# Token phase of a streaming encoder step: the queues of its stores, the unit in which its keys are transposed, and the tiles of the rotation's scratch

## The chip, the core and the metric

The kernel runs on one core of a Trainium2 chip. The metric is the device time of one execution in microseconds (us), as a median of several runs. Work is spread over TensorE (PE; PEld is its weight load), VectorE (DVE), ScalarE (ACT), GpSimd (POOL) and SyncE (SP). Each engine takes its instructions in a fixed order, and a transfer is started by an instruction in the queue of SP, ACT or POOL.

## The reference, cut to what matters

One layer over 4096 prompt frames and 32 sample frames, all in float32:

```python
h = rmsnorm(x, norm_g)
proj = jnp.einsum('bsd,de->bse', h, w_in)
q, k, v, ga, u, gp = jnp.split(proj, [...], axis=-1)
q = rope(q.reshape(B, S, N_HEADS, 2, HEAD_DIM), pos)      # 4 heads, two 64-wide halves each
k = rope(k.reshape(B, S, N_HEADS, 2, HEAD_DIM), pos)      # k and v are outputs too
o = diff_attention(q, k_all, v_all, pos, kpos_all, lam)   # block-causal
o = rmsnorm(o, subln_g, SUBLN_EPS) * (1.0 - lam_init)
a_out = o.reshape(B, S, ATTN_WIDTH) * jax.nn.silu(ga)
p_out = pool_mix(u, pool_hist, pos, w_pool, pool_scale) * jax.nn.silu(gp)
y = x + jnp.einsum('bse,ed->bsd', jnp.concatenate([a_out, p_out], axis=-1), w_out)
y = rmsnorm(y, final_g)
```

Outputs are y, the rotated keys, the values and the last pooling rows, for the prompt and for the sample.

## The kernel before, in words

Four phases follow each other: the token phase (`token_phase`: queries, keys and values of all tokens), the channel phase (gates and pooling), attention, and the output projection. Only the token phase is touched by the change; in the profile it lies between 0 and about 560 us. What it makes goes to scratch in DRAM, from where attention loads it.

A float32 product is made of three matmuls over a high and a low part of each operand (`mm3`, L112 to L114), so a projection over the 1024 inputs is 8 steps of three matmuls. Tokens come in nine spans (`SPANS`, mostly 512 tokens, four blocks of 128). For each span there are units of 24 matmuls: four q units, then a k unit for each block, then a v unit for each block. A unit writes a PSUM tile of the pool `two`, which has three buffers (`bank`), so the PSUM tile of a unit must have been read before the third unit after it can start.

The steps that the prediction speaks of:

- `norm_in`, `norm`: a block of rows is loaded (xn, L247), ACT squares and sums it (L252), DVE makes the reciprocal of the mean (L253, L254), and ACT its root (rx, L255). `scales_out` (L259) writes the 128 values of a block, one from each partition, to `rx_scr`; `scales` (L221) reads them back spread over all partitions (bc).
- `x_parts` loads two 128-row pieces of the transposed input (x, L205), and ACT and DVE split them (L108, L109). `ahead` places these loads and splits of the next span among the units of the current one.
- `q_out`: DVE scales the sums (z, L275), rotates the first tile with the help of two ACT copies (L278, L279), ACT and DVE split it into hi and lo, and both are stored (L288).
- `keys_out`: ACT scales the sums into kt (L299), POOL rotates 16 of each 64 columns in place (L304 to L307, with the scratch rot), and kt is stored (L308). `keys_across`: PE transposes kt in four pieces into the one PSUM tile `tp` (L314), ACT and DVE split it (L108, L109), and hi and lo are stored (L319).
- `values_out`: ACT scales the sums into v (L325), which is stored twice (L326, L327).
- `load_piece` (L237 to L239): a piece of weights is loaded, and ACT and DVE split it.

A k unit or a v unit begins with six of its eight steps, then calls `across` (which transposes all keys held so far) and ends with the two last steps. So the keys of a unit are transposed within the unit that follows it.

All stores and loads of this phase are started from SP. The tiles kt, rot, hi, lo, z, zs, v and bc share the eight buffers of one tag of the pool `sm`; the row and input tiles (xn, x before its split, tab) share four buffers of the pool `st`. The framework orders each engine's instructions when the program is built. The transfers of SP (and of ACT, where it starts any) share eight completion semaphores, and a transfer that is given one waits at its queue's head until the previous transfer on it has landed; POOL's transfers have others.

Of the kernel before, what the change touches and what calls it, by code (L numbers as in the profile page):

```python
# [11 lines left out]
F32 = mybir.dt.float32  # L12
# [8 lines left out]
P = 128  # L21
# [6 lines left out]
NB = SEQ // P  # L28
NH = 4
# [38 lines left out]
def encoder(tc, a, o):  # L68
    nc = tc.nc
    V, S, G, T = nc.vector, nc.scalar, nc.gpsimd, nc.tensor  # L70
    dma = nc.sync.dma_start
    rdma = nc.gpsimd.dma_start
    with ExitStack() as es:
        def pool(name, bufs, **kw):
            return es.enter_context(tc.tile_pool(name=name, bufs=bufs, reuse_waits="tile", **kw))
# [9 lines left out]
        q_scr = dram.tile([NH * 2, 2, 64, TOK], F32R, name="q_scr")  # L85
        rx_scr = dram.tile([1, TOK], F32, name="rx_scr")
        k_scr = dram.tile([NH, 2, 2, 64, TOK], F32R, name="k_scr")
        v_scr = dram.tile([NH, P, NB + 1, P], F32, name="v_scr")
# [12 lines left out]
        def s_tile(shape, dt=F32, name="s"):  # L101
            return sm.tile(shape, dt, tag="s", name=name)
# [4 lines left out]
        def split(hi, lo, src):  # L107
            S.copy(hi, src)  # L108
            V.tensor_sub(lo, src, hi)  # L109
# [9 lines left out]
        def p2_tile(name):  # L119
            return two.tile([P, 1024], F32, tag="two", name=name)  # L120

        def p1_tile(tag, name):
            return one.tile([P, 512], F32, tag=tag, name=name)
# [36 lines left out]
        etiny = early.enter_context(tc.tile_pool(name="etiny", bufs=2, reuse_waits="tile"))  # L160
        cs = econst.tile([P, NB + 1, 2, 8], F32, name="cs")
        rx = const.tile([P, NB + 1], F32, name="rx")
# [62 lines left out]
        def token_phase():  # L225
# [15 lines left out]
            def blocks(sp):  # L241
                t0, n = sp[:2]
                return [(t, min(P, t0 + n - t)) for t in range(t0, t0 + n, P)]
# [12 lines left out]

            def scales_out(t0, n):
                for t, m in blocks((t0, n)):
                    dma(rx_scr[0:1, t:t + m].rearrange("o t -> t o"), rx[:m, t // P:t // P + 1])  # L259

            def table(t0, n):
                tab = st.tile([P, 2, 512], F32, tag="st", name="tab")
# [8 lines left out]
            def q_out(ps, sp, i, bc, tab):  # L271

                t0, n = sp[:2]
                z = s_tile([P, 512], name="z")
                V.scalar_tensor_tensor(z[:, :n], ps[:, :n], 0.125, bc[:, :n], op0=ALU.mult, op1=ALU.mult)  # L275
                if i == 0:
                    zs = s_tile([P, 512], name="zs")
                    S.copy(zs[0:64, :n], z[64:128, :n])  # L278
                    S.copy(zs[64:128, :n], z[0:64, :n])  # L279
                    V.tensor_mul(z[:, :n], z[:, :n], tab[:, 0, :n])  # L280
                    V.tensor_mul(zs[:, :n], zs[:, :n], tab[:, 1, :n])
                    V.tensor_add(z[:, :n], z[:, :n], zs[:, :n])
                hi = s_tile([P, 512], F32R, name="hi")
                lo = s_tile([P, 512], F32R, name="lo")
                split(hi[:, :n], lo[:, :n], z[:, :n])
                for l, t in ((0, hi), (1, lo)):
                    for p0, p1, d in ((0, 64, 0), (64, 128, 8)) if i == 0 else ((0, P, i * 16),):
                        dma(q_scr[:, l, d:d + (p1 - p0) // 8, t0:t0 + n].rearrange("g d t -> g d t").bitcast(F32),  # L288
                            t[p0:p1, :n].bitcast(F32))

            def project(ps, sp, t0, m, kind, k):
                c = slice(t0 - sp[0], t0 - sp[0] + m)
                xh, xl = sp[2:4]
                mm3(ps[:m], xh[k][:, c], xl[k][:, c], w[kind][k][0], w[kind][k][1], k == 0, k == NK - 1)

            def keys_out(ps, t0, m):
                b = t0 // P
                kt = s_tile([P, 512], name="kt")
                S.activation(kt[:m], ps[:m], AF.Copy, scale=rx[:m, b:b + 1])  # L299
                ab = kt[:m].rearrange("t (g d) -> t g d", d=64)[:, :, 0:16].rearrange("t g (z f) -> t g z f", z=2)  # L300
                rot = s_tile([P, 2, 8, 2, 8], name="rot")
                rc, rs = rot[:m, 0], rot[:m, 1]
                bc = lambda i: cs[:m, b, i].unsqueeze(1).unsqueeze(1).to_broadcast([m, 8, 2, 8])
                G.tensor_mul(rc, ab, bc(0))  # L304
                G.tensor_mul(rs, ab, bc(1))
                G.tensor_sub(ab[:, :, 0], rc[:, :, 0], rs[:, :, 1])
                G.tensor_add(ab[:, :, 1], rc[:, :, 1], rs[:, :, 0])  # L307
                dma(o["k_prompt"][t0:t0 + m, :] if b < NB else o["k_sample"], kt[:m])  # L308
                return t0, m, kt

            def keys_across(t0, m, kt):
                tp = p1_tile("tp", "tp").rearrange("p (h t) -> p h t", h=NH)
                for h in range(NH):
                    T.transpose(tp[:, h, :m], kt[:m, h * P:(h + 1) * P], ident[:m, :m])  # L314
                hi = s_tile([P, NH, P], F32R, name="hi")
                lo = s_tile([P, NH, P], F32R, name="lo")
                split(hi[:, :, :m], lo[:, :, :m], tp[:, :, :m])
                for l, t in ((0, hi), (1, lo)):
                    dma(k_scr[:, l, :, :, t0:t0 + m].rearrange("h j d t -> (j d) h t").bitcast(F32),  # L319
                        t[:, :, :m].bitcast(F32))  # L320

            def values_out(ps, t0, m):
                b = t0 // P
                v = s_tile([P, 512], name="v")
                S.activation(v[:m], ps[:m], AF.Copy, scale=rx[:m, b:b + 1])  # L325
                dma(o["v_prompt"][t0:t0 + m, :] if b < NB else o["v_sample"], v[:m])  # L326
                dma(v_scr[:, :m, b].rearrange("h t e -> t h e"), v[:m].rearrange("t (h e) -> t h e", h=NH))  # L327

            def bank():
                return p2_tile("ps")[:, 0:512]  # L330

            held = []

            def across():
                while held:
                    keys_across(*held.pop(0))

            def q_unit(sp, i):
                ps = bank()
                for k in range(NK):  # L340
                    q_sum(ps, sp, i, k)
                q_out(ps, sp, i, *sp[4])

            def k_unit(sp, t):
                ps = bank()
                for k in range(NK):
                    if k == 6:
                        across()
                    project(ps, sp, *t, 1, k)
                held.append(keys_out(ps, *t))  # L350

            def v_unit(sp, t):
                ps = bank()
# [25 lines left out]
            def run(units, *jobs):  # L379
                for u, unit in enumerate(units):  # L380
                    for j in jobs:
                        for f in j.pop(u, []):
                            f()
                    unit()
                for j in jobs:
                    for u in sorted(j):
                        for f in j[u]:
                            f()


            t0, n = SPANS[0]
# [18 lines left out]
            bl = blocks(sp)  # L410
# [9 lines left out]
            both = p2_tile("ps")  # L420
# [3 lines left out]
            for t, xn in zip(bl, xns):  # L424
                norm(*t, xn)
            scales_out(t0, n)
            for k in range(NK):
                load_piece(2, k)
            for i in range(2):
                held.append(keys_out(both[:, i * 512:i * 512 + 512], *bl[i]))  # L430

            def rest():
                extra.extend([scales(t0, n), table(t0, n)])
# [6 lines left out]
            for s in range(1, len(SPANS) - 2):  # L440
# [7 lines left out]
                bl = blocks(sp)  # L448
# [174 lines left out]

        channel = channel_phase()
        last_channels = channel.send(token_phase())


# [358 lines left out]
        def out_half(yp, w, hl, m, n, k):  # L986
            r = slice(n * 512, (n + 1) * 512)
            mm3(yp[:m, :512], hl[:, 0, k, :m], hl[:, 1, k, :m], w[k][0][:, r], w[k][1][:, r], k == 0, k == 3)

        class PoolPart:  # L990
# [26 lines left out]
            def unit(self):  # L1017

                t0, m, hl, xn = self.blocks[0]
                if self.x == 0:  # L1020
                    self.yp = p2_tile("yp")
                for x in range(self.x, self.x + UNIT):
                    out_half(self.yp[:, x // 4 * 512:], self.w, hl, m, x // 4, x % 4)
                    if x == 7:
                        V.tensor_add(xn[:m], self.yp[:m], xn[:m])  # L1025
                self.x = (self.x + UNIT) % 8
                self.left -= 1
                if self.x == 0:
                    dma(x_scr[t0:t0 + m, :], xn[:m])
                    self.blocks.pop(0)  # L1030
                    if self.seq:
                        self.blocks.append(self.load())
                return UNIT * 0.64
# [185 lines left out]
```

## Time and profile before

| what | us |
|---|---|
| median of 3 runs (2866.47 to 2874.34) | 2867.46 |
| the profiled execution | 2871.01 |
| its span | 2869.2 |
| PE busy in the span (97%) | 2769.3 |
| PE waiting between 40 and 500 us, all of it for a key's tile or its bank | 48.2 |

The page's first part has PE busy in 97% of the span, and its second part shows the slices in which it was not. The share is a mean over four phases, so the stretch of the token phase is to be read by itself. A time in the rows is counted from the span's start.

### The profile page before, as it was taken

How to read it: one execution, taken by the hardware profiler on the slowest of the kernel's cores; microseconds unless marked ns; L12 is line 12 of the kernel's file. 1: busy time of each engine (PE TensorE's matmuls, PEld its weight loads, DVE VectorE, ACT ScalarE, POOL GpSimd, SP SyncE). 2: the span in 40 equal slices, each digit the busy share in tenths (PEclk: the TensorE clock that was granted, in tenths of full speed). 3: DMA queues.
4: the chain of work that ended last, by engine and by line, in shares of the span. 5: the costliest groups of instructions: out<-in, count | busy, mean ns of one | idle time of the engine just before them, and what ended most of it. 6: DMA issues, size and time to landing. Idle time of an engine off the chain costs nothing. (4 is left out here: it accounts for less than half of the span.)

```text
span 2869.2 us, 42987 instructions
## 1 busy us (share of the span) xinstructions
PE 2769.3 (97%) x15719; PEld 2361.0 (82%) x15719; DVE 1839.7 (64%) x3543; ACT 1615.5 (56%) x3403; POOL 247.4 (9%) x507
## 2 busy tenths in 40 slices
PE   7699999999999999999999999999999989999998
PEld 6577778878888889888888788888888878888776
DVE  4322222235555555787888778788888878888666
ACT  5332222232222221378877777777888878888553
POOL 0000000010000011210001000011000110000000
PEclk9899999999999999999999999999999999999999
DMA  8787666562333333842336535356333451213873
GB/s 246 185 197 166 167 176 161 170 212 92 114 111 113 115 98 85 214 93 58 79 73 126 109 90 114 74 105 134 75 72 73 88 105 26 59 30 91 293 256 131
DMA packets 281427, 356.87 MB, mean 124 GB/s; under 512 B 29800, under 2 KB 192864, under 8 KB 280448
## 3 DMA queue, kind: packets, MB, share of 16 engines
q1 hardware_dynamic: 206608, 278.49, 33.2%
q0 software_dynamic: 74608, 75.64, 15.3%
q8 instruction: 124, 2.03, 0.3%
q14 instruction: 87, 0.71, 0.1%
HBM read 218.77 MB, written 135.28 MB: 123 GB/s over the span
## 5 line engine op out<-in xcount | busy, mean ns | idle before, releaser
L647 DVE TENSOR_REDUCE nm<-sc 128x1 f32<-128x1024 f32 (+8 forms) x612 | 636.7, 1045 | 112.0 <-PE sc L750 105.5
L750 PE MATMUL sc<-kv,qt 128*128 128x512 f32 (+2 forms) x2304 | 669.6, 404 | 23.9 <-ACT p L656 14.1
L778 PEld LDWEIGHTS av<-kv,at 128*128 128x128 f32 x4224 | 548.9, 191 | 31.6 <-DVE ot L784 1.5
L778 PE MATMUL av<-kv,at 128*128 128x128 f32 x4224 | 573.9, 275 | 0.5 <-ACT at L697 0.2
L750 PEld LDWEIGHTS sc<-kv,qt 128*128 128x128 f32 x2304 | 389.7, 191 | 98.0 <-ACT p L656 40.9
L112 PE MATMUL ps<-x,w 128*128 128x512 f32 (+2 forms) x1152 | 423.7, 368 | 7.6 <-ACT x L108 6.5
L113 PE MATMUL ps<-x,w 128*128 128x512 f32 (+2 forms) x1152 | 423.4, 368 | 0.0
L114 PE MATMUL ps<-x,w 128*128 128x512 f32 (+2 forms) x1152 | 423.3, 367 | 0.1
L697 ACT COPY at<-tp 128x512 f32<-128x512 f32 (+3 forms) x579 | 318.5, 550 | 159.2 <-PE tp L694 154.9
L656 ACT ACTIVATE p<-sc,nm 128x1024 f32<-128x1024 f32 (+7 forms) x386 | 360.3, 935 | 69.8 <-DVE nm L647 67.1
L688 DVE SCALAR_TENSOR_TENSOR p<-p,c 128x1024 f32<-128x1024 f32 (+5 forms) x322 | 344.2, 1080 | 2.3
L694 PE MATMUL tp<-ident,p 128*128 128x128 f32 x2121 | 332.3, 274 | 4.2 <-ACT at L697 3.5
L656 ACT ACTIVATE p<-sc,ref 128x1024 f32<-128x1024 f32 (+7 forms) x258 | 262.6, 1019 | 68.3 <-DVE ref L651 49.6
L694 PEld LDWEIGHTS tp<-ident,p 128*128 128x128 f32 x2121 | 251.0, 141 | 45.2 <-ACT at L697 19.1
L112 PEld LDWEIGHTS ps<-x,w 128*128 128x128 f32 x1152 | 217.0, 188 | 43.8 <-ACT x L108 6.5
L113 PEld LDWEIGHTS ps<-x,w 128*128 128x128 f32 x1152 | 217.1, 188 | 36.0 <-DVE x L109 0.4
L114 PEld LDWEIGHTS ps<-x,w 128*128 128x128 f32 x1152 | 217.1, 188 | 35.7 <-DVE w L239 0.5
L112 PE MATMUL yp<-wo,hl 128*128 128x512 f32 (+1 forms) x528 | 221.7, 420 | 8.8 <-DVE xn L1025 3.4
L112 PE MATMUL ps<-w,x 128*128 128x512 f32 (+1 forms) x528 | 214.2, 406 | 10.3 <-ACT kt L299 10.3
L113 PE MATMUL ps<-w,x 128*128 128x512 f32 (+1 forms) x528 | 210.6, 399 | 0.0
L114 PE MATMUL ps<-w,x 128*128 128x512 f32 (+1 forms) x528 | 210.4, 398 | 0.0
L113 PE MATMUL yp<-wo,hl 128*128 128x512 f32 (+1 forms) x528 | 208.8, 396 | 0.0
(154 smaller groups left out, 3135.2 us busy)
## 6 DMA issues: line engine op xcount, KB each, us to landing
xn<-xn SPq DMA_DIRECT2D x64, 512.0 KB
qt<-q_scr POOLq DMA_DIRECT2D x128, 256.0 KB, 4.2
x<-xT SPq DMA_DIRECT2D x56, 512.0 KB
hl<-gp_scr POOLq DMA_DIRECT2D x32, 512.0 KB, 5.3
kv<-k_scr POOLq DMA_DIRECT2D x32, 512.0 KB, 10.1
x_scr<-xn SPq DMA_DIRECT2D x32, 512.0 KB
xn<-x_scr SPq DMA_DIRECT2D x32, 512.0 KB
y_prompt<-xn SPq DMA_DIRECT2D x32, 512.0 KB
```

The lines of the kernel that those rows point to most:

```text
L112: T.matmul(ps, lh, rh, start=first, stop=False)
L113: T.matmul(ps, lh, rl, start=False, stop=False)
L114: T.matmul(ps, ll, rh, start=False, stop=last)
L647: V.tensor_reduce(ref if self.ng == 1 and j else bias, sc, axis=AX.X, op=ALU.max, negate=True)
L656: S.activation(p[:, :w], sc, AF.Exp, bias=bias, accum_out=self.l[:, j, g:g + 1])
L688: V.scalar_tensor_tensor(p1[:, :w], p2[:, :w], self.c[:, g:g + 1], p1[:, :w], op0=ALU.mult, op1=ALU.add)
L694: T.transpose(tp[:blk.shape[1], i], blk, ident)
L697: S.copy(at[:r, :n], tp[:r, :n])
L750: T.matmul(sc[:, off:off + pw], qt[:, j, x, q0:q0 + P], keys[:, kk:kk + pw], start=x == 0, stop=x == 1)
L778: T.matmul(self.av[:, 0:P], self.at[:, i], self.value(kb), start=self.blk == 0, stop=self.blk == self.qb)
```

## The change

Three edits, all in the token phase. (1) Stores move to other queues. Those of rx, of the hi part of queries and keys, and both of v are started from ACT, whose queue also holds the instruction that made the tile. The store of kt is started from POOL, after the rotation. The lo parts, made by DVE, stay on SP, and so do all loads. (2) Keys are held for a unit longer: those of unit u are transposed in unit u + 2. (3) The rotation's scratch has two tiles of its own in `etiny` instead of one of the eight of `sm`.

```diff
+    adma = nc.scalar.dma_start
             def scales_out(t0, n):
                 for t, m in blocks((t0, n)):
-                    dma(rx_scr[0:1, t:t + m].rearrange("o t -> t o"), rx[:m, t // P:t // P + 1])
+                    adma(rx_scr[0:1, t:t + m].rearrange("o t -> t o"), rx[:m, t // P:t // P + 1])
...
-                        dma(q_scr[:, l, d:d + (p1 - p0) // 8, t0:t0 + n].rearrange("g d t -> g d t").bitcast(F32),
+                        (dma if l else adma)(q_scr[:, l, d:d + (p1 - p0) // 8, t0:t0 + n].rearrange("g d t -> g d t").bitcast(F32),
                             t[p0:p1, :n].bitcast(F32))
...
-                rot = s_tile([P, 2, 8, 2, 8], name="rot")
+                rot = etiny.tile([P, 2, 8, 2, 8], F32, name="rot")
...
-                dma(o["k_prompt"][t0:t0 + m, :] if b < NB else o["k_sample"], kt[:m])
+                rdma(o["k_prompt"][t0:t0 + m, :] if b < NB else o["k_sample"], kt[:m])
...
-                    dma(k_scr[:, l, :, :, t0:t0 + m].rearrange("h j d t -> (j d) h t").bitcast(F32),
+                    (dma if l else adma)(k_scr[:, l, :, :, t0:t0 + m].rearrange("h j d t -> (j d) h t").bitcast(F32),
...
-                dma(o["v_prompt"][t0:t0 + m, :] if b < NB else o["v_sample"], v[:m])
-                dma(v_scr[:, :m, b].rearrange("h t e -> t h e"), v[:m].rearrange("t (h e) -> t h e", h=NH))
+                adma(o["v_prompt"][t0:t0 + m, :] if b < NB else o["v_sample"], v[:m])
+                adma(v_scr[:, :m, b].rearrange("h t e -> t h e"), v[:m].rearrange("t (h e) -> t h e", h=NH))
...
-            held = []
+            held, unit_no = [], [0]
             def across():
-                while held:
-                    keys_across(*held.pop(0))
+                while held and held[0][0] < unit_no[0] - 1:
+                    keys_across(*held.pop(0)[1])
...
-                held.append(keys_out(ps, *t))
+                held.append((unit_no[0], keys_out(ps, *t)))
...
                     unit()
+                    unit_no[0] += 1
...
-                held.append(keys_out(both[:, i * 512:i * 512 + 512], *bl[i]))
+                held.append((i - 1, keys_out(both[:, i * 512:i * 512 + 512], *bl[i])))
```

The order on PE in the k units of the second span, before. ps_974 is the PSUM tile of its second k unit, kt_960 the keys of its first:

```order
L112 MATMUL ps_974<-w_292,x_649 128x512
L113 MATMUL ps_974<-w_292,x_649 128x512
L114 MATMUL ps_974<-w_292,x_650 128x512
L314 MATMUL tp_993<-ident_92,kt_960 128x128 x4
L112 MATMUL ps_974<-w_292,x_690 128x512
L113 MATMUL ps_974<-w_292,x_690 128x512
L114 MATMUL ps_974<-w_292,x_691 128x512
```

The same keys after the change; ps_1013 is the PSUM tile of the third k unit:

```order
L113 MATMUL ps_1013<-w_292,x_638 128x512
L114 MATMUL ps_1013<-w_292,x_638 128x512
L115 MATMUL ps_1013<-w_292,x_639 128x512
L315 MATMUL tp_1032<-ident_92,kt_960 128x128 x4
L113 MATMUL ps_1013<-w_292,x_690 128x512
L114 MATMUL ps_1013<-w_292,x_690 128x512
```

PE now has one more unit of 24 matmuls ahead of these transposes. Outside the token phase the order of no engine differs.

The order on SP at the program's start, before (ident and what follows it; wst is a piece of weights, tab the table of the queries' rotation):

```order
L413 DMA ident<-ident 128x128
L259 DMA rx_scr<-rx 128x1 x3
L263 DMA tab<-rope 128x2x512
L237 DMA wst<-w_in 128x512
L259 DMA rx_scr<-rx 128x1
L237 DMA wst<-w_in 128x512 x7
L247 DMA xn<-xn 128x1024
L205 DMA x<-xT 128x2x512
```

And after the change, as far as the first load of bc:

```order
L416 DMA ident<-ident 128x128
L264 DMA tab<-rope 128x2x512
L248 DMA xn<-xn 128x1024
L238 DMA wst<-w_in 128x512 x8
L206 DMA x<-xT 128x2x512
L248 DMA xn<-xn 128x1024
L206 DMA x<-xT 128x2x512
L482 DMA icnt<-icnt 128x64
L487 DMA shist<-spT 128x4x15
L248 DMA xn<-xn 128x1024
L206 DMA x<-xT 128x2x512
L222 DMA bc<-rx_scr 128x512
```

The stores of rx are gone from between the loads. Before, bc came after five loads and seven stores of keys that follow the last of these weights; now it comes after five loads of rows and inputs and two small ones.

The order on ACT around the first keys of the second span (kt_960), before:

```order
L108 CAST hi_923<-z_921 128x512
L252 ACTIVATE xn_1259,ss_101<-xn_1259 128x1024
L299 ACTIVATE kt_960<-ps_935,rx_100 128x512
L255 ACTIVATE rx_100<-ss_101 128x1
L108 CAST hi_998<-tp_993 128x512
```

And after the change:

```order
L109 CAST hi_923<-z_921 128x512
L253 ACTIVATE xn_1421,ss_101<-xn_1421 128x1024
L289 DMA q_scr_75<-hi_923 8x16x512
L256 ACTIVATE rx_100<-ss_101 128x1
L260 DMA rx_scr_76<-rx_100 128x1
L300 ACTIVATE kt_960<-ps_935,rx_100 128x512
L300 ACTIVATE kt_999<-ps_974,rx_100 128x512
L109 CAST hi_1037<-tp_1032 128x512
L320 DMA k_scr_77<-hi_1037 128x4x128
```

ACT now starts stores between its casts, and three blocks of the next span's rows (the last is xn_1421) are squared ahead of these keys, where it was one (xn_1259).

## Rows read from the trace of the kernel before

**Rows 1.** Busy time of each engine in stretches of 100 us.

```profile
core 0: us, PE busy (x) PEld busy (x) DVE busy (x) ACT busy (x) POOL busy (x), PEclk, DMA share, GB/s
0.00:100.00 100.00, 73.75 (x302) 58.58 (x303) 38.49 (x67) 48.77 (x83) 7.59 (x31) 0.90 0.82 236
100.00:200.00 100.00, 83.73 (x367) 68.94 (x366) 24.59 (x48) 31.85 (x54) 5.89 (x16) 0.91 0.84 185
600.00:700.00 100.00, 99.98 (x442) 80.12 (x441) 52.73 (x77) 29.55 (x39) 5.52 (x7) 1.00 0.45 144
```

**Rows 2.** PE's waits between 40 and 500 us: in total, times, the longest.

```profile
PE tp L314 <- POOL kt L307: 37.7, 7, 16.3
PE ps L112 <- ACT kt L299: 10.3, 1, 10.3
```

**Rows 3.** PE by time: start, length, operation, tiles, shapes, [wait <- releaser].

```profile
54.47 1.11 PE L314 MATMUL tp<-ident,kt 128*128 128x128 f32 x4 [8.76 <-POOL kt L307]
...
85.90 0.79 PE L112 MATMUL ps<-w,x 128*128 128x512 f32 x1 [10.31 <-ACT kt L299]
...
148.20 1.12 PE L314 MATMUL tp<-ident,kt 128*128 128x128 f32 x4 [16.27 <-POOL kt L307]
148.97 0.78 PE L112 MATMUL ps<-w,x 128*128 128x512 f32 x1
...
152.53 0.63 PE L114 MATMUL ps<-w,x 128*128 128x512 f32 x1
...
222.68 1.12 PE L314 MATMUL tp<-ident,kt 128*128 128x128 f32 x4 [4.77 <-POOL kt L307]
```

**Rows 4.** The engines in three short stretches, columns as in the first group.

```profile
28.00:44.00 16.00, 16.00 (x73) 13.23 (x72) 0.32 (x2) 3.19 (x7) 0.00 (x0) 1.00 0.77 84
92.00:100.00 8.00, 8.00 (x37) 6.63 (x36) 0.00 (x0) 0.69 (x1) 0.00 (x0) 1.00 0.99 301
140.00:150.00 10.00, 1.80 (x7) 1.61 (x8) 0.35 (x3) 2.42 (x6) 1.46 (x4) 0.50 0.71 224
```

**Rows 5.** ACT in order of time, ahead of the three waits.

```profile
44.36 0.72 ACT L238 ACTIVATE w<-wst,gcol 128x512 fp32r<-128x512 f32 x1 [9.38 <-DMA wst<-w_in]
...
52.13 0.67 ACT L299 ACTIVATE kt<-ps,rx 128x512 f32<-128x512 f32 x1
...
85.16 0.69 ACT L299 ACTIVATE kt<-ps,rx 128x512 f32<-128x512 f32 x1 [0.67 <-DVE lo L109]
...
134.57 1.04 ACT L108 CAST x<-x 128x1024 fp32r<-128x1024 f32 x1 [10.15 <-DMA x<-xT]
...
145.86 0.67 ACT L299 ACTIVATE kt<-ps,rx 128x512 f32<-128x512 f32 x1
```

**Rows 6.** SP in order of time: issues, their length, and how many.

```profile
23.73 3.92 SPq L259 DMA_DIRECT2D rx_scr<-rx  x3
...
28.86 0.54 SPq L237 DMA_DIRECT2D wst<-w_in  x1
...
63.08 0.40 SPq L221 DMA_DIRECT2D bc<-rx_scr  x1
...
74.67 1.36 SPq L288 DMA_DIRECT2D q_scr<-hi  x2
...
95.96 0.35 SPq L326 DMA_DIRECT2D v_prompt<-v  x1
...
123.52 0.47 SPq L205 DMA_DIRECT2D x<-xT  x1
...
126.80 3.38 SPq L259 DMA_DIRECT2D rx_scr<-rx  x4
```

**Rows 7.** DVE: the first scaled queries of the first span.

```profile
68.85 0.69 DVE L275 SCALAR_TENSOR_TENSOR z<-raw,bc 128x512 f32<-128x512 f32 x1 [5.47 <-DMA x<-xT]
```

**Rows 8.** The longest of ACT's waits for rows, between 40 and 500 us.

```profile
ACT xn L252 <- DMA xn<-xn: 77.8, 22, 10.8
```

**Rows 9.** POOL: two issues of loads in the channel phase.

```profile
1034.70 1.42 POOL L726 DMA_DIRECT2D qt<-q_scr  x2 [3.14 <-DVE x L109]
```

## The prediction

> **What bounds the kernel now.** I began with the busy time of the engines by stretches of 100 us, because the page's 97% for PE is a mean over four phases. Outside the token phase there is nothing to win: in the channel phase PE is busy for 99.98 us of 100, at a granted clock of 1.00 [rows 1]. Whatever PE saves earlier is therefore handed on to the end us for us, and whatever it loses is paid for in full. In the first two hundred us PE is busy for 73.8 and 83.7 of 100 [rows 1]. The list of PE's waits shows what the gaps are: seven waits of the transposes for POOL's rotated keys, 37.7 us, and one wait of a first matmul for its bank, 10.3 us [rows 2]. DVE and ACT are busy for less than half of any of these stretches [rows 1]; they are late, not full. So I followed each large wait back, in order of time, through PE, ACT, DVE and SP.
>
> T1, 8.8 us at 54.47 [rows 3]. The keys' tile was made on ACT at 52.13 only, because ACT, in order, had stood 9.4 us before a split of weights at 44.36 [rows 5]. That piece was started at 28.86, behind three stores of rx, whose issue alone took 3.92 us [rows 6].
>
> T2, 10.3 us at 85.90, for a bank that ACT's kt at 85.16 frees [rows 3, 5]. It ends a chain: bc is loaded from 63.08 [rows 6], the first z can run at 68.85 [rows 7], and 16.3 us of scaling, splitting and copying in ACT's and DVE's order later comes that kt.
>
> T3, 16.3 us at 148.20 [rows 3]. ACT waited 10.2 us for an input piece that was started at 123.52 and split at 134.57; four stores of rx took 3.38 us of SP's time from 126.80 [rows 5, 6]. ACT's waits for rows are as long: 77.8 us in 22, up to 10.8 [rows 8]. The keys were scaled at 145.86 [rows 5].
>
> T4, the other five: 37.7 − 8.8 − 16.3 = 12.6 us, the largest 4.8, at 222.68 [rows 2, 3].
>
> Behind a wait PE is slow for a while. From 140 to 150 us its granted clock is 0.50, the lower level, 1.2 GHz [rows 4]; after T3 the start of one matmul and that of the ninth behind it lie 152.53 − 148.97 = 3.56 us apart [rows 3], where a steady stretch has 442 matmuls in 100 us, .226 us each [rows 1], so 2.03 for nine. A restart costs 1.5 us.
>
> **The change part by part.** *Transposes a unit later.* A unit is 24 matmuls, 24 × .226 = 5.4 us. Nothing is added to PE: the same four transposes stand after another six steps. The slack between a unit's sums and the use of its keys grows by 5.4 us, more than the largest of T4. By this edit alone T4 goes (12.6), and T1 and T3 would shrink to 3.4 and 10.9. A kt lives 5.4 us longer in the eight shared buffers; the scratch rot leaves them at the same time, so I take nothing for buffers. If the scratch's own two tiles make POOL wait, it is for its own earlier work, in order, so nothing again. Where keys come due in pairs, at the head of the first span, two sets go through the one tile tp and PE waits for its split: some 1 us in all, by the .69 us that an operation on 512 columns takes on ACT [rows 5].
>
> *Stores of rx, hi and v to ACT, of kt to POOL.* For SP this removes the 3.92 and 3.38 us blocks of rx from between the loads [rows 6], and, more than that, the waiting: a store at the head of SP's queue waits for its tile, and the loads behind it with it. In the new order bc stands before all stores of keys, where seven stood before it.
>
> For ACT it adds 163 issues in the token phase: 28 of rx at 3.38 / 4 = .85, 36 of q hi at 1.36 / 2 = .68, 99 of k hi and v, which I take at v's .35 [rows 6]: 24 + 24 + 35 = 83 us. These prices are SP's; ACT starts nothing here before. From below it costs nothing that PE sees, since ACT is busy for 49 and 32 of 100 us in the first two stretches [rows 1] and 83 over some 560 us are 15 per 100. From above, each issue that falls between a unit's end and its kt delays the keys; the new 5.4 us covers some seven of them. I take nothing, but for T2's chain. For POOL it adds 33 issues; two of its loads took 1.42 us [rows 9], so .7 each, 23 us in all against 6 to 8 busy us per 100 [rows 1], behind the rotation: nothing.
>
> What ACT now does first also counts. Three blocks of the next span's rows are squared ahead of the second span's first keys, where it was one. A square takes some 1 us but waits for its rows, up to 10.8 us [rows 8]. If the loads come early, as I expect, two more squares and the stores between cost 3 to 4 us, inside the new slack; if not, see the rivals.
>
> *T1 and T3* both begin with a load that SP started late or that landed slowly. With one unit more of slack T1 needs its weights 3.4 us earlier and T3 its input 10.9 us earlier. For T1 the 3.92 us of the rx issues are enough by themselves. For T3 the four issues give 3.38, and the rest must come from loads that no longer wait behind stores. I take both as gone; the bound on the other side is that they shrink by the slack only.
>
> *T2* I leave at 10.3. Its 16.3 us chain from z to kt stays, and ACT's issues lengthen it; bc is earlier, by the seven stores, but PE reaches the same bank 8.8 + 1.5 us sooner as T1 is gone. The bounds: it grows by these 10.3 if the chain stays where it is, and goes if bc comes 20 us sooner.
>
> *The pace of the transfers.* Their engines are busy for .82 and .84 of the first two hundred us, 166 us of full work [rows 1]. The gain takes about 28 us out of this stretch, which leaves 172: a share of .97. The fullest row shown is .99, over 8 us at 301 GB/s [rows 4], so that it holds for 170 us is not shown. I charge 5 us, an estimate; zero if the work itself shrinks, 12 if a mean share of .9 is all there is (166 / .9 = 184).
>
> There is a row that speaks against the first edit. From 28 to 44 us the transfers' engines are busy for .77 of the time and move 84 GB/s, against 301 at a share of .99 [rows 4]: the stores of rx are in flight there, 128 values from 128 partitions each. If it is the transfer and not its issue that holds up the weights, another queue changes nothing for the loads.
>
> The Trainium skill says so (DMA: Bandwidth & Descriptors, Issuing engines are not separate DMA queues): all queues run on the same 16 engines, and spreading transfers over issuing engines saves only issue time. By that rule it would be the first rival's 2844.5 below. The same page (Queues, rings and completion order) has each engine take turns between the queues' rings, a packet at a time, so that a load is not behind all of another queue's writes; by that, the forecast. No run here shows which.
>
> The sum: all seven waits for keys 37.7, and six restarts at 1.5, 9.0; less 1 for the pairs and 5 for the transfers: 40.7. The profiled execution took 2871.0, so 2830.3; the median of the runs is 3.5 below it: 2826.8, say **2827**.
>
> **The rivals.** *A: the loads land no earlier.* The transfers' engines are the limit in the first 150 us. For it: the 84 GB/s at .77, and an input that took 11 us [rows 4, 5]. Against it: 301 GB/s where loads and stores run freely [rows 4]. Then T1's 5.4 are lost again in T2, whose chain hasn't moved; T3 gives 5.4, T4 12.6, four restarts 6, less 1: 23. That is 2844.5.
>
> *B: slower. ACT's queue blocks.* A transfer that ACT starts may have to wait at the head of ACT's queue for an earlier one, a load of SP's among them, since they share eight completion semaphores; behind it on ACT stand the kt and the v that free PE's banks. The longest wait for a load is 10.8 us [rows 8]. If each of eight spans has one such block ahead of its keys, PE waits 10.8 − 5.4 + 1.5 = 6.9 us a span, 55 us; T4 and its restarts (18.6) are gone, T1 and T3 stay: 2867.5 + 36 = 2904. It turns slower once such a block passes 5.4 − 1.5 + 18.6 / 8 = 6.2 us in the mean. Against it: the loads are started ahead of their use, waits for keys in the later spans are 4.8 us at most [rows 3], and the stores that ACT and POOL start no longer stand in front of SP's loads.
>
> *C: no change to speak of.* The two extra squares and the stores on ACT take the new slack, T4 goes, but T2 grows by as much: within 9 us of 2867.5.
>
> **How the numbers follow.** Forecast .58, A .27, B .08, C .07. A difference of 0.3%, 8.6 us, is about what a measurement of this kernel can tell from no change. Both the forecast and A are faster by more: .85; C is the same: .07, B slower: .08. The range: the best case has no wait left, 37.7 + 10.3 and eight restarts of 1.5, so 60 off 2867.5: 2807.5; I begin a little above, at 2812, as the transfers then run at over .99. Upward it includes A with the 7 us more that a mean share of .9 would cost, 2851.5, and ends at 2853. B, C and a tail of A lie outside.
>
> **What would show it.** PE's waits between 40 and 500 us should hold one large entry, for a bank near 75 to 86 us, and at most 6 us for keys. From 28 to 44 us the transfers should move well over 150 GB/s and the weights be split before 42. If instead the weights are split at about 44 again, A holds; the sign of it is T3 at about 11. ACT should issue its stores in .35 to .85 us each with no long waits in its queue; if ACT's waits for transfers of its own sum to over 30 us between the spans, B holds. POOL's issues should be about .7 us behind the rotation. From the channel phase on everything should be as before, only earlier. The forecast is wrong if T2 more than doubles, or if a new wait of PE for v or z appears, of which before shows none.

## The result, and the profile after

The changed kernel takes 2890.5 us (median of 4 runs, 2888.9 to 2891.5) against 2868.7 for the kernel before in the same comparison: a ratio of 1.0072, 95% interval 1.0055 to 1.0090. I had forecast 2827. It is slower, by 22 us, and the profiled execution agrees: its span is 2889.3 us, 20.1 more than before.

PE's own work did not grow (2771.3 us busy, before 2769.3). The loss is waiting, in the same stretch. These are PE's waits of the changed kernel between 40 and 500 us, with the columns of [rows 2]:

```profile
PE tp L315 <- DVE lo L110: 25.7, 2, 25.2
PE tp L315 <- POOL kt L308: 22.4, 2, 11.8
PE ps L113 <- DVE z L276: 22.0, 7, 7.2
PE tp L315 <- DVE ss L254: 0.6, 1, 0.6
PE ps L113 <- ACT v L326: 0.2, 1, 0.2
```

They sum to 70.9 us, where it was 48.0 [rows 2]: 23 more, all of it before 200 us (from 200 to 500 us they are 12.3 us in both kernels). In order of time (columns as in [rows 3]), in the first two spans:

```profile
61.40 1.12 PE L315 MATMUL tp<-ident,kt 128*128 128x128 f32 x4 [10.53 <-POOL kt L308]
...
101.29 1.09 PE L315 MATMUL tp<-ident,kt 128*128 128x128 f32 x4 [25.21 <-DVE lo L110]
...
160.54 0.79 PE L113 MATMUL ps<-w,x 128*128 128x512 f32 x1 [7.23 <-DVE z L276]
...
178.44 1.12 PE L315 MATMUL tp<-ident,kt 128*128 128x128 f32 x4 [11.84 <-POOL kt L308]
```

T1 did not go: 10.5 us, where 8.8 stood. T2, which I left at 10.3, is 25.2, and is now a wait of the second keys' transposes for the tile tp, whose last contents DVE splits only after the queries. T3 shrank from 16.3 to 11.8, but 7.2 us for a bank come ahead of it. Only T4 behaved as expected, and there too waits for banks took its place.

Behind T1, T2 and T3 are late loads. The windows answer to those of [rows 1] and [rows 4], with the same columns; first the changed kernel, then two windows of the kernel before:

```profile
0.00:100.00 100.00, 58.96 (x244) 47.85 (x244) 36.93 (x70) 46.51 (x79) 8.31 (x31) 0.84 0.87 203
100.00:200.00 100.00, 75.87 (x319) 60.58 (x320) 18.95 (x35) 26.04 (x46) 10.16 (x25) 0.88 0.79 170
20.00:30.00 10.00, 10.00 (x46) 8.28 (x45) 5.45 (x9) 4.68 (x9) 0.00 (x0) 1.00 0.85 108
28.00:44.00 16.00, 16.00 (x72) 13.23 (x72) 3.12 (x9) 7.62 (x16) 0.00 (x0) 1.00 1.04 244
40.00:50.00 10.00, 10.00 (x45) 8.28 (x45) 4.19 (x6) 3.29 (x6) 0.00 (x0) 1.00 0.88 58
```

```profile
20.00:30.00 10.00, 10.00 (x46) 8.29 (x45) 6.68 (x13) 6.88 (x14) 0.00 (x0) 1.00 0.76 236
40.00:50.00 10.00, 5.71 (x26) 4.39 (x24) 4.62 (x7) 4.76 (x7) 0.00 (x0) 1.00 0.76 185
```

In the first 100 us the transfers moved 203 GB/s at a share of .87; before it was 236 at .82. There are stretches in which their engines are nearly full and move little, 58 GB/s at .88 from 40 to 50 us, where it was 185 at .76. From 28 to 44 us, where the prediction looked for its sign, they do move more, 244 GB/s instead of 84; the slow stretches now lie on both sides of it. Next ACT and DVE, where the stores of rx went and what came late (first column the start; ACTq is ACT's queue of issues):

```profile
35.60 0.33 ACTq L260 DMA_DIRECT2D rx_scr<-rx  x1
...
37.19 0.33 ACTq L260 DMA_DIRECT2D rx_scr<-rx  x1
...
45.28 0.33 ACTq L260 DMA_DIRECT2D rx_scr<-rx  x1
...
56.09 0.72 ACT L239 ACTIVATE w<-wst,gcol 128x512 fp32r<-128x512 f32 x1 [2.38 <-DMA wst<-w_in]
...
173.91 1.06 ACT L253 ACTIVATE xn<-xn 128x1024 f32<-128x1024 f32 x1 [12.68 <-DMA xn<-xn]
```

```profile
73.61 0.69 DVE L276 SCALAR_TENSOR_TENSOR z<-raw,bc 128x512 f32<-128x512 f32 x1 [8.63 <-DMA bc<-rx_scr]
...
92.13 0.69 DVE L110 TENSOR_TENSOR lo<-z,hi 128x512 fp32r<-128x512 f32 x1 [4.90 <-DMA q_scr<-lo]
...
98.37 0.69 DVE L110 TENSOR_TENSOR lo<-z,hi 128x512 fp32r<-128x512 f32 x1 [3.68 <-DMA q_scr<-lo]
...
100.45 0.69 DVE L110 TENSOR_TENSOR lo<-tp,hi 128x512 fp32r<-128x512 f32 x1 [1.13 <-DMA xn<-xn]
```

These issues of rx take ACT .33 us each. But the last weights are split at 56.1 us, when before they were done in time for a kt at 52.1 [rows 5]. They were not started later. These are the issues and the splits of the weights with their first and last start, first before, then after the change, and the issue of bc after it:

```profile
L237 SPq DMA_DIRECT2D wst<-w_in x24: 327/328/939, 1.2 to 46.9; - x24
L238 ACT ACTIVATE w<-wst,gcol x24: 707/720/725, 5.2 to 51.5; 128x512 fp32r<-128x512 f32 x24
```

```profile
L238 SPq DMA_DIRECT2D wst<-w_in x24: 327/328/1496, 1.2 to 45.9; - x24
L239 ACT ACTIVATE w<-wst,gcol x24: 707/710/725, 5.3 to 56.1; 128x512 fp32r<-128x512 f32 x24
...
61.34 0.46 SPq L222 DMA_DIRECT2D bc<-rx_scr  x1
```

The last weight starts 1.0 us earlier and is split 4.6 us later. bc starts 1.7 us earlier than before [rows 6], yet the first z waits for it until 73.6, 4.8 us later than the first z before [rows 7]; then DVE waits 4.9 and 3.7 us for buffers whose stores have not landed. In the second span the square ahead of the keys waits 12.7 us for its row.

### The profile page after: what moved, and what is told of

Its sections match the earlier page's. It is cut to its first block, busy times and chain, and to the rows that moved or that the text cites. A ratio compares the mean times of both kernels' runs of the same rounds, so it can differ in the third digit from the quotient of the medians.

```text
span 2889.3 us, 42900 instructions
## 1 busy us (share of the span) xinstructions
PE 2771.3 (96%) x15719; PEld 2362.8 (82%) x15719; DVE 1839.0 (64%) x3543; ACT 1616.1 (56%) x3403; POOL 266.5 (9%) x540
```

## The experiments

Theory L was that rx's stores, on a queue of their own beside the loads, make the loads land later. Theory P, its rival, was that the later transposes stand in a bad place, behind the queries. All ratios are to the kernel before, in the same comparison (2868 to 2870 us), with their 95% intervals.

**Which edit.** Four kernels: the queues alone, the later transposes alone, the changed kernel with rx back on SP, and rx on ACT as the only edit.

```diff
# rx on ACT alone
-                    dma(rx_scr[0:1, t:t + m].rearrange("o t -> t o"), rx[:m, t // P:t // P + 1])
+                    adma(rx_scr[0:1, t:t + m].rearrange("o t -> t o"), rx[:m, t // P:t // P + 1])
# the changed kernel with rx on SP: this line the other way round
# the queues alone: all dma -> adma, rdma of the change, nothing else
# the later transposes alone: held, unit_no and across as changed, nothing else
```

> Only the stores move to other queues; keys are transposed in the next unit as before, and the scratch stays in its old pool. Theory P (place): what costs is the later transposes, since the split of the first keys comes to stand behind the queries' outputs on DVE. Then this kernel keeps PE's wait near 86 us at about 10 and is no slower than before: 2855 to 2870 us. Theory L (loads): what costs is that the stores of rx run on a queue of their own beside the loads, so that weights and bc land later. Then this kernel is slower than before by 10 us or more (2880 to 2895), the last weights are split after 54 us (before: 51.5), bc takes about 12 us to land (before: under 6), and from 40 to 50 us the transfers move well under 185 GB/s.

> Only the transposes come a unit later; all stores stay on SP. Theory P: the first keys' split stands behind the queries' outputs, so the wait of PE at 76 us grows from 10.3 towards 20, while the wait before it (8.8) shrinks by up to 5.4, the one at 148 by 5.4, and the five small ones go: 2850 to 2865 us by these alone, and 2880 or more only if the place by itself explains the changed kernel. Theory L: this kernel has before's loads, so it is faster than before by about the slack gained, 12 to 25 us: 2845 to 2857.

> The changed kernel, but the stores of rx stay on SP; the other stores, the later transposes and the scratch's tiles as changed. Theory L: the weights and bc land as before, and the gain of the later transposes shows: 2845 to 2865 us. Theory P: nothing of the loss comes from rx, so within 5 us of the changed kernel's 2890.

> The kernel before with one edit: the stores of rx start from ACT. Theory L: 8 to 20 us slower than before (2876 to 2888), with the last weights split after 54 us and bc's landing at 10 us or more. Theory P: the loads of SP no longer stand behind 3.9 and 3.4 us of issues, so it is within 5 us of before or a little faster.

| kernel | us | ratio |
|---|---|---|
| queues alone | 2915.2 | 1.0157 (1.0136 to 1.0178) |
| later transposes alone | 2861.2 | .9972 (.9961 to .9984) |
| changed, rx on SP | 2866.0 | .9993 (.9979 to 1.0008) |
| rx on ACT alone | 2927.8 | 1.0215 (1.0197 to 1.0233) |

One line of the change costs 59 us by itself, three times what theory L allowed; the rest of the change gives part of it back. Theory L has the sign of the loss right and misses its range in all four kernels, by 1 to 40 us. P falls as an explanation of the loss: the queues alone are slower, and the later transposes alone a little faster, within its 2850 to 2865 us. Its wait is real, though: 15.7 us for DVE's split at 86 us in that kernel, 26.7 at 92 with rx on SP. How rx does its harm is seen in the kernel with rx on ACT alone: first its windows, then ACT.

```profile
54.00:60.00 6.00, 0.00 (x0) 0.00 (x0) 2.15 (x4) 3.63 (x6) 1.20 (x2) 0.50 0.79 280
62.00:70.00 8.00, 7.45 (x28) 5.57 (x27) 1.31 (x2) 0.58 (x1) 1.16 (x2) 0.80 0.76 48
70.00:72.00 2.00, 0.00 (x0) 0.00 (x0) 0.00 (x0) 0.07 (x1) 0.00 (x0) 1.00 0.78 296
```

```profile
60.46 0.33 ACTq L260 DMA_DIRECT2D rx_scr<-rx  x1
...
71.94 1.06 ACT L253 ACTIVATE xn<-xn 128x1024 f32<-128x1024 f32 x1 [9.35 <-DMA xn<-xn]
```

A single store of 128 values leaves at 60.5; by the packet records its own packets are over by 61.5. From 62 to 70 us everything in flight, loads and stores, moves at 48 GB/s with the engines busy for .76; after that 296 GB/s again, and the awaited row lands.

**Together or apart.** The same values in one store for a span (from ACT, and from SP), or in four stores from ACT issued together; and no stores of rx at all, in both kernels, with bc loaded from a row of the input instead.

```diff
# one store
+                if n % P == 0:
+                    adma(rx_scr[0:1, t0:t0 + n].rearrange("o (b p) -> p (o b)", p=P), rx[:, t0 // P:(t0 + n) // P])
# four together
+                four = etiny.tile([P, 4], F32, name="four")
+                S.copy(four[:, :n // P], rx[:, b0:b0 + n // P])
...
+                    adma(rx_scr[0:1, t:t + m].rearrange("o t -> t o"), four[:m, i:i + 1])
# none (in the changed kernel the stores taken out are adma)
-                for t, m in blocks((t0, n)):
-                    dma(rx_scr[0:1, t:t + m].rearrange("o t -> t o"), rx[:m, t // P:t // P + 1])
+                pass
...
-            dma(bc[:, :n], rx_scr[0:1, t0:t0 + n].to_broadcast([P, n]))
+            dma(bc[:, :n], a["xT"][0:1, t0:t0 + n].to_broadcast([P, n]))
```

> The kernel before with rx stored from ACT, but one store for a span (512 values from 128 partitions) in place of four of 128. The four stores from ACT, each on its own, made 2928 us. Theory S (separate stores): every rx store that is alone in flight opens some 8 us in which the transfers move 15 to 65 GB/s, whatever its size; four apart cost four such stretches a span, four together one or two. Then this kernel has one stretch a span and is at 2855 to 2870. Theory Q (queue): what costs is that a queue of its own mixes the small writes in among the loads; then the same 512 writes cost the same, and it is at 2910 or more.

> The kernel before with one store of rx for a span in place of four, left on SP. If the queue by itself matters little, it is within 8 us of the same store from ACT, 2852.6. If ACT's queue is the worse place whatever the number, it is 10 us or more below that; if it blocks SP's loads, 10 us or more above.

> The kernel before with rx stored from ACT in four stores of 128 values a span, as in the kernel of 2928 us, but all four issued together: ACT first copies the span's four columns of rx into a tile of its own, and the four stores read that. Theory S (a stretch of slow transfers opens for each store or group that is alone in flight): the group of four costs about what one store did, 2852 to 2872 us. Theory C (each store costs, wherever its neighbours are): four times as many stores as the kernel of 2853, so 2905 to 2930.

> The kernel before without any store of rx: bc is loaded, as much and as often, from a row of the transposed input instead, so that queries and gates get another scale. Both theories S and Q: the stretches of under 90 GB/s between 28 and 44 us go, and the waits of PE at 54, 86 and 148 us shrink: 10 to 35 us faster than before, 2835 to 2858. If it stays within 5 us of before, the small writes are not what holds up the loads, and both fall.

> The changed kernel without any store of rx, bc loaded from a row of the transposed input (queries and gates get another scale). If the stores of rx are the whole reason for the loss, this is no slower than before without them and shows the gain that I forecast: 2825 to 2845 us. If the other moved stores or the place of the first keys' split cost as well, a wait of 10 us or more stays between 70 and 100 us and the time is above the same kernel without the moves.

| stores of rx for a span | us | ratio |
|---|---|---|
| four from ACT, each as it is ready | 2927.8 | 1.0215 (1.0197 to 1.0233) |
| four from ACT, together | 2879.5 | 1.0053 (1.0034 to 1.0072) |
| four from SP (the kernel before) | 2868.7 | 1 |
| one from SP | 2862.3 | .9976 (.9959 to .9992) |
| one from ACT | 2852.6 | .9941 (.9920 to .9963) |
| none | 2824.2 | .9838 (.9814 to .9861) |
| none, in the changed kernel | 2817.9 | .9819 (.9796 to .9843) |

From ACT, issuing the same four stores together gives back 48 of the 104 us between the first row and "none"; making one of four, 27 more; the last 28 are the price of the one. The time of the four together lies between what theories S and C expected. It does not show a price of the number, though, because the four did not always run together. Of those issued at 197.9 us, ACT's queue ran 432 packets in 198 to 203 us and 144 in 207 to 210:

```profile
q10 hardware_dynamic: 432, 0.00, 4.8%
```

```profile
q10 hardware_dynamic: 144, 0.00, 2.7%
```

So theory S, with two slow stretches in such a span, is not excluded.

From SP four stores or one differ by 6 us only, from ACT by 75; ACT is 10 us better than SP for one store and 59 worse for four that leave as they are ready. This is not only because SP issues rx in threes and fours. It does so up to 130 us [rows 6]; from 150 us on it issues them in ones and twos as well, and yet PE's waits between 200 and 500 us are short in the kernel before (first line) and long with rx on ACT alone (second):

```profile
PE tp L314 <- POOL kt L307: 12.1, 4, 4.8
PE tp L315 <- POOL kt L308: 42.7, 4, 11.6
```

The changed kernel with rx back on SP issues them in ones and twos, too, but for three at 23 us, and it is 24 us faster than the changed kernel (2866.0 to 2890.5). One of the single stores of the kernel before, and the window behind it:

```profile
190.15 0.33 SPq L259 DMA_DIRECT2D rx_scr<-rx  x1
...
191.00:199.00 8.00, 8.00 (x37) 6.63 (x36) 3.81 (x5) 2.29 (x3) 0.00 (x0) 1.00 1.03 172
```

So coming apart is dear on ACT's queue and hardly on SP's. Why, these runs do not show.

Without rx stores both kernels came out faster than expected. The changed one is faster than the other: 2817.9 against 2824.2 in the same comparison, and each of its four runs (2816.7 to 2820.6) lies below each of the other's five (2821.0 to 2829.5). So some 6 us are left of the gain of 40 that I forecast. The windows of the changed kernel without them, beside those above:

```profile
0.00:100.00 100.00, 83.64 (x349) 67.81 (x350) 45.94 (x86) 58.58 (x101) 10.32 (x35) 0.93 0.86 285
20.00:30.00 10.00, 10.00 (x46) 8.28 (x45) 6.97 (x15) 8.17 (x16) 0.00 (x0) 1.00 0.94 325
40.00:50.00 10.00, 10.00 (x46) 8.29 (x45) 3.93 (x7) 6.55 (x11) 4.91 (x9) 1.00 0.72 241
```

At the same share as the changed kernel (.86 and .87) they move 285 GB/s instead of 203, and PE is busy for 84 us instead of 59.

**Traffic or waiting, and what in it.** Leaving the stores out also took away the wait of bc for them. So: the stores stay, apart and from ACT, but nobody reads them; and the same with 512 bytes from each partition instead of 4.

```diff
# unread: rx on ACT as above, and
+            dma(bc[:, :n], a["xT"][0:1, t0:t0 + n].to_broadcast([P, n]))
# 512 bytes each: that, but in place of the store of rx
+                    wide = etiny.tile([P, P], F32, name="wide")
+                    S.copy(wide[:m], rx[:m, t // P:t // P + 1].to_broadcast([m, P]))
+                    adma(rx_wide[t:t + m, :], wide[:m])
```

> The kernel before with the stores of rx from ACT, each on its own, as in the kernel of 2928 us; but nobody reads what they store: bc is loaded from a row of the transposed input (queries and gates get another scale). Theory T (traffic): the stores slow the other transfers while they are in flight; then it stays near 2928, 2905 to 2935. Theory W (wait): what costs is that the load of bc must wait for the last of these stores to land; then it is near the kernel without them, 2824 to 2835.

> As the last one, but each of these unread stores writes 512 bytes from each partition, 64 KB, in place of 4 bytes (ACT first spreads the column of rx over 128 columns of a tile). Theory V (value): it is the writes of single values that slow the others; then 128 times the bytes cost less, and it is at 2824 to 2845. Theory N (number): any small store on its own does; then it stays at 2900 or more.

Unread: 2931.3, 1.0222 (1.0199 to 1.0245). With 512 bytes each: 2827.4, .9858 (.9836 to .9880). It is the traffic, not the waiting; and the same number of stores with 512 bytes from each partition costs almost nothing. The two differ in a second thing: 128 single values lie side by side in 512 bytes of `rx_scr`, the wide rows 512 bytes apart in `rx_wide`. Whether it is the size of a write or that so many go to one place, this pair does not tell. From 62 to 70 us, the unread kernel and then the wide one:

```profile
62.00:70.00 8.00, 6.74 (x27) 5.08 (x26) 0.81 (x2) 0.08 (x1) 0.65 (x2) 0.86 0.48 36
```

```profile
62.00:70.00 8.00, 5.70 (x26) 4.38 (x24) 5.00 (x11) 6.09 (x13) 0.00 (x0) 1.00 0.59 198
```

The queues' table says who pays (packets, MB, share of 16 engines' time, 0 to 500 us; q1 is SP's queue, q10 ACT's). The unread kernel, then the kernel before with none:

```profile
q1 hardware_dynamic: 64790, 82.58, 71.8%
q10 hardware_dynamic: 4347, 0.02, 0.6%
```

```profile
q1 hardware_dynamic: 82198, 97.95, 61.8%
```

The small packets themselves take .6% by the record. The others become longer: .87% per MB on q1 where it is .63% without.

The Trainium skill (DMA: Bandwidth & Descriptors, Specifications) gives 512 B as the least size for full rate and says that below it the engine reads, modifies and writes. The pair of runs agrees as far as it goes, 4 bytes 2931 us and 512 bytes 2827; no size between was run.

**The place of the first split, and versions to keep.** The later transposes alone, with the first span's query outputs called two units later; the changed kernel with one store of rx; the changed kernel with bc made by TensorE and stored as one row; and that with the query outputs later, too.

```diff
# query outputs later
-                extra.extend([scales(t0, n), table(t0, n)])
...
-            jobs[1].insert(0, rest)
+            jobs[1].insert(0, lambda: extra.extend([scales(t0, n), table(t0, n)]))
+            jobs[3].insert(0, rest)
# bc by TensorE, for the load of bc and the stores of rx
+                for t, m in blocks((t0, n)):
+                    T.transpose(tp[:, t - t0:t - t0 + m], rx[:m, t // P:t // P + 1].to_broadcast([m, P]), ident[:m, :m])
+                bc = s_tile([P, 512], name="bc")
+                S.copy(bc[:, :n], tp[:, :n])
+                dma(rx_scr[0:1, t0:t0 + n], bc[0:1, :n])
```

> The transposes a unit later as the only edit of the change, and the first span's four query outputs called two units later, so that the splits of its first keys come ahead of them on ACT and DVE; bc is still loaded where it was. Theory P for this one wait: the 15.7 us at 86 us, for DVE's split, go, and some 10 to 17 us of the time: 2845 to 2853 against 2861 with the queries first. If PE merely waits as long for something else of that chain (a bank, a buffer whose store has not landed), it is within 4 us of 2861.

> The changed kernel with one edit: rx goes out in one store for a span, from ACT. The kernel before was 28 us slower with that one store than with none (2852.6 against 2824.2), and the changed kernel with none took 2817.9: so about 2846, 2835 to 2852. If the moved stores of hi, v and kt or the later transposes suffered under it by themselves, it would not be faster than 2853.

> The changed kernel, but TensorE makes bc: four transposes of a column of rx spread over 128 columns into the PSUM tile tp, a copy by ACT into SBUF, and one store of one partition's 512 values as a row, for the channel phase. No store of single values is left. By the kernel without stores of rx, 2817.9, plus 33 transposes of some .28 us on PE, 9 us: 2827, range 2818 to 2838. If a row's store holds up the transfers like the others, 2845 or more.

> As the last one, with the first span's query outputs called two units later, after the splits of its first keys. If PE's wait for that split (7.8 us in the changed kernel without stores of rx) goes with it, 4 to 9 us below the last one; if that wait only changes its cause, the same within 3 us.

| kernel | us | ratio |
|---|---|---|
| later transposes, query outputs later | 2856.5 | .9963 (.9948 to .9979) |
| changed, one store of rx | 2835.8 | .9894 (.9877 to .9911) |
| changed, bc by TensorE | 2822.7 | .9848 (.9828 to .9868) |
| the same, query outputs later | 2820.4 | .9846 (.9826 to .9865) |

Calling the queries later removes the 15.7 us wait, but waits of 5.4, 1.5 and 6.6 us come in the same span; the ratio is not told apart from .9972. So the place of the split decides which wait is long and not, measurably, the time. The one store came out 10 us better than worked out from the kernel before. With bc from TensorE PE has one wait over a microsecond left between 40 and 500 us:

```profile
PE tp L323 <- DVE lo L110: 10.2, 1, 10.2
```

This kernel computes all of the reference and beats the kernel before by 1.5% and the changed one by 2.3% (2890.5 to 2822.7). The query outputs later add nothing that the intervals show.

## Why the prediction was wrong

*What bounds the kernel* was right: after 500 us nothing changed, and the loss passed to the end unchanged (23 us more waiting, 20 more span).

*The step that failed* is the first edit's: "For SP this removes the 3.92 and 3.38 us blocks of rx from between the loads [rows 6], and, more than that, the waiting". I put the late loads down to when SP started them. SP did start them earlier, the last weight by 1.0 us and bc by 1.7, and they were there later, by 4.6 and 4.8. They were late because of how slowly they moved once started: the stores of rx, small as they are, slowed everything in flight. The row was in the prediction, 84 GB/s at .77 [rows 4], and I gave it to rival A, with .27. A was right about the cause, that the transfers and not their issue hold the weights, and wrong in its price, because it took the traffic as fixed. The edit changed the traffic: from ACT each store left by itself as its block was ready. This move alone costs 59 us, and taking it back gives the changed kernel 24. Up to 130 us SP had issued them in threes and fours; that this is what spared the kernel before is not shown, since later single stores from SP did little harm. No rival had the loads move more slowly than before, so the measured time lay outside the range.

*T1 and T3* were therefore not gone but 10.5 and 11.8. Without rx stores they are gone in the kernel before already: 37.7 us of waits for keys become 7.3 (four waits, the longest 3.4).

*T2* I left at 10.3, with 10.3 more as the upper bound. It took 14.9 more: the first z, waiting for bc, ran 4.8 us later where I expected it earlier, and the changed order put the split that PE waits for behind all four query outputs and their buffers. The order showed that place, and I priced only the pairs there, at 1 us.

*T4*: 12.6 us gone, as forecast, but 12.3 us of waits for banks that z frees came in the later spans (3.9, 3.2, 2.1 and 3.1). The later transposes alone show no wait from 200 to 500 us, and neither does the changed kernel without rx stores; with rx on SP and the other stores moved there are three such waits, 7.1 us.

*ACT's cost and rival B*: ACT issued rx 33 times, mostly in .33 us, where I took 28 times .85. Its waits for stores that it had started itself come to some 25 us between 40 and 500 us, the longest 6.4, and only .2 us of PE's waits are for v. B had the right sign through another mechanism; its loads did arrive late (a square waited 12.7 us), but the waits traced above go back to loads and stores that landed late, not to ACT's queue.

*The transfers' pace* I charged at 5 us on a share that was to rise. It stayed at .87 and .79; it was the work done at that share that fell. One reading in the sum was off without weight: in [rows 3] the matmul at 152.53 is the eighth behind the one at 148.97, so a restart is 1.75 us and not 1.5.

## What to carry to other kernels

When the transfers' engines are busy and few bytes move, look for stores of single values among them, and price them by what they do to the transfers beside them, not by their bytes or issue time. Before a small store is moved to another queue, try that move alone: here it cost 59 us, with nothing in its own records to show for it. Stores of the same values that leave together, or as one, cost less on that queue. A column of values that others need as a row is better turned by TensorE and stored as a row: here 33 transposes, 9 copies and 9 stored rows took the place of 33 stores of single values and of 9 loads.

## What the runs showed of the hardware

A store of 128 values of 4 bytes takes ACT .33 us to issue. In the two kernels with rx on ACT that are shown at 62 to 70 us, everything in flight behind such a store moves at 36 to 48 GB/s for 8 us; with 512-byte pieces it is 198 in the same window. Not every store does as much: with rx on ACT alone, the 8 us that begin 1 us after a single store moved 59 to 205 GB/s before 150 us (median 73) and 72 to 201 after it (median 138, where the mean of that stretch is 156). After 150 us, those behind the single stores that SP issues in the kernel before moved 53 to 219 (median 164, mean 172).

Over the token phase, 33 such stores from ACT, apart, cost 104 us against none, four together a span 55, one a span 28 (38 from SP), and 512-byte pieces in their place 3, which is within the intervals of none. The records of the small packets show nothing of this; it appears as longer packets of the other queue. Not shown by these runs is why a small write holds up its neighbours, why single ones do so more from ACT's queue than from SP's, and whether the size counts or that the values lie side by side.
